# Three gate projections behind the context's norm, and the conditioning vector in the context's buffer

## The chip, the cores and the metric

The kernel runs on one core of a Trainium2 chip. The metric is the device time of one execution in microseconds (us). The engines of the core work side by side, each through its own list of instructions in order: TensorE (PE in the profile), VectorE (DVE), ScalarE (ACT), GpSimd (POOL) and SyncE (SP), which here only issues transfers. An instruction waits until what it needs has been written and until the buffer that it writes has been read for the last time.

## The reference, cut to what matters

One block of a diffusion transformer for 1024 tokens of width 1024, with a context of 256 tokens. The context is normalized and gives keys and values; the tokens give a long convolution, queries, keys, values and two gates, all from one weight matrix `w_in`.

```
ada   = silu(c) @ w_ada + b_ada                      # conditioning, 6 x 1024
hc    = modulate(rmsnorm(ctx, g_mix_pre), csh1, csc1)
kv_c  = hc @ w_in[:, OFF_K:OFF_G]                    # context keys and values
h     = modulate(rmsnorm(x, g_mix_pre), sh1, sc1)
proj  = h @ w_in
y_hy  = hyena_branch(proj[..., :OFF_Q], *hy_p) @ w_hy_up
q, k, v from proj; k_all = [k, k_c]; v_all = [v, v_c]
y_att = heads_out(diff_attention(q, k_all, v_all, lam)) @ w_att_up
g_hy, g_att = split(sigmoid(proj[..., OFF_G:]), 2)   # the gates: 2 x 1024 columns
mixed = (g_hy * y_hy + g_att * y_att) @ w_out
x = x + g1 * rmsnorm(mixed, g_mix_post); then the gated feed-forward layer
```

## The kernel before, in words

Matrices lie with their 128 rows of a tile on the partitions. A projection of 128 columns is a *tile* of `w_in`: `wload` (L126) loads 128x1024 weights from HBM (SP queue, L123), ScalarE casts them to the rounded form `whi`, VectorE subtracts to get the rest `wlo`, and `proj` (L136) does 24 matmuls per half of the tokens (8 each of `h_hi,whi`, `h_hi,wlo`, `h_lo,whi`). Buffers for `wraw`, `whi` and `wlo` are two each, so at most two tiles of weights are on their way. `raw_tile` (L486) projects one tile for both halves (48 matmuls) and stores it to HBM; the 16 gate tiles are such tiles (`graw`, tiles 24 to 39 of `win`).

The stages, by the time of the profile: the filter and the norm of the tokens (to 165 us), the Hyena convolutions (to about 525 us), the context stage (to about 614 us), the attention of four heads with the projections of the next head between (to about 1015 us), the mixing, the output and the feed-forward layer (to 1855 us).

Each of the four convolutions calls `filler` (L626) six times: in its forward transform twice, after the first and second product with the filter's spectrum, after finish(0) and finish(2), and after finish(1) and finish(3). Each call emits one tile. There are 24 tiles in the list, 8 of the convolution's own inputs and 16 gates, so the last three calls of the last convolution emit gate tiles 13, 14 and 15; the loop at L642 finds the list empty. `finish` (L578) does four matmuls, a copy by ScalarE (`yt`), four transposes and a product by VectorE into `u`. `hyena_out` (L605) casts `u` and stores it as `zs`.

The context stage (L743 to L772): `cx` is loaded on ScalarE's queue, squared and summed; `ss` sums over the partitions with TensorE (L170); VectorE forms the inverse root in twelve small operations and the diagonal `dg`; `bc` spreads it with TensorE (L184); VectorE multiplies and modulates `cx` and splits it into `c_hi` and `c_lo`. Then come q, k and v of head 0, the keys and values of the context for the four heads (24 matmuls of 256 columns each), and 15 conditioning tiles (`ada_tile`, L148): each loads 128x1024 of `w_ada` and reduces it against the vector `sc2` with one VectorE instruction. `sc2` is silu(c) on all partitions (`silu_bc`, L144). Context projections take their PSUM tile from a pool of two.

What sets the order is not the text alone: a scheduler orders each engine's instructions by its own costs, so that a tile that is written later can run earlier on its engine where nothing forbids it. SP's queue is one list too: a load that stands behind a store is issued only when the store's data is there.

Of the kernel before, what the change touches and what calls it, by code (L numbers as in the profile page):

```python
# [9 lines left out]
F32 = mybir.dt.float32  # L10
# [7 lines left out]
P = 128  # L18

L, D, C, DFF = 1024, 1024, 256, 2816  # L20
KD = D // P
# [12 lines left out]
NS, NTR = 3, 2  # L34
NHY = 6
FILL3 = ((10, 0), (1, 11), (2, 12), (3, 4, 5))
NGT = 16
NAB = 2
NGB = 12
UPO = (0, 0, 1, 1)  # L40
# [24 lines left out]
def block_kernel(tc, xT, ctxT, cvec, cT, wada1, wada, vecs, lamv, dbias, zT, fw1, fw2, fv, fw3, decay, mfs, mis, rope,  # L65
                 win, wup, wout, wgate, wupf, wdown, outT):
    nc = tc.nc
# [14 lines left out]
    def tt(out, a, b, op, eng=None):  # L82
        (eng or V).tensor_tensor(out=out, in0=a, in1=b, op=op)  # L83
# [7 lines left out]
    def act(out, in_, func, bias=0.0, scale=1.0, **k):  # L91
        A.activation(out=out, in_=in_, func=func, bias=bias, scale=scale, **k)

    def f(ap):
        return ap.bitcast(F32)

    def rawdma(out, in_, eng=None):
        (eng or nc.sync).dma_start(out=f(out) if out.dtype == F32R else out,
                                   in_=f(in_) if in_.dtype == F32R else in_)
# [4 lines left out]
    def pool(name, bufs=1, side=None, **k):  # L104
        return tc.tile_pool(name=name, bufs=bufs, side=side, **k)
# [20 lines left out]
    def wload(src, nk=8, neng=None):  # L126
        return wsplit(wload_raw(src, nk), nk, neng)
# [8 lines left out]
    def proj(ps, whi, wlo, xs, start=True, stop=True):  # L136
        n = len(xs)
        seq = [(whi, 0, k) for k in range(n)] + [(wlo, 0, k) for k in range(n)] + [(whi, 1, k) for k in range(n)]
        for i, (w, j, k) in enumerate(seq):
            T.matmul(out=ps, lhsT=w[:, k * P:(k + 1) * P], rhs=xs[k][j],  # L140
                     start=start and i == 0, stop=stop and i == len(seq) - 1)


    def silu_bc(dst, eng=None):  # L144
        (eng or nc.sync).dma_start(out=dst, in_=cvec.broadcast_to([P, D]))
        act(dst, dst, AF.Silu)
# [339 lines left out]
    def raw_tile(m, dst, ps_tile=None, gt_tile=None):  # L486
        whi, wlo = wload(win[m])
        for n in range(2):
            ps = ps_tile() if ps_tile else pacc.tile([P, 512], F32, tag="acc", name="ps")
            proj(ps, whi, wlo, hx[n])  # L490
            gt = gt_tile() if gt_tile else gpl.tile([P, 512], F32, tag="gt", bufs=2, name="gt")
            A.copy(out=gt, in_=ps)  # L492
            nc.sync.dma_start(out=dst[:, n * 512:(n + 1) * 512], in_=gt)
# [32 lines left out]
    matrices(mi, mis, lambda: yp.tile([P, 1024], F32, tag="hk", bufs=NHK, name="mraw"))  # L526

    def fftconv(u, o, c, p, filler):

        by_r = lambda t: t.rearrange("p h (a r) -> p h r a", r=8)  # L530
        S, D_ = quad(), quad()
        for r in (0, 2, 1, 3):
            pt = psf()
            for j, rr in enumerate((r, r + 4)):
                for h in range(2):
                    T.transpose(out=pt[:, j * 256 + h * P:j * 256 + (h + 1) * P], in_=by_r(u)[:, h, rr], identity=ident)
            ut = yp.tile([P, 512], F32, tag="ut", bufs=NUT, name="ut")
            A.copy(out=ut, in_=pt)
            pp = []
            for j in range(2):  # L540
                ps = psf()
                for part in range(2):
                    T.matmul(out=ps[:, part * 256:(part + 1) * 256], lhsT=mf[:, r + 4 * j, part],  # L543
                             rhs=ut[:, j * 256:(j + 1) * 256], start=True, stop=True)
                pp.append(ps)
            sd_from_psum(pp[0], pp[1], S, D_, SLOT[r])
            if r in (2, 3):
                filler()
# [14 lines left out]
        dft8_even(S, -1, Ze)  # L563
        times_k(Ze, 0)
        filler()
        Zo = quad()
        dft8_odd(D_, -1, Zo)
# [37 lines left out]
    def hyena_out(c, z):  # L605
        for h in range(2):
            hi = yp.tile([P, L], F32R, tag="hk", bufs=NHK, name="zhi")
            lo = yp.tile([P, L], F32R, tag="hk", bufs=NHK, name="zlo")
            A.copy(out=hi, in_=z[:, h])
            tt(lo, z[:, h], f(hi), ALU.subtract)  # L610
            rawdma(zs[0][c * 2 + h], hi)
            rawdma(zs[1][c * 2 + h], lo)
# [10 lines left out]

    tiles = [(m, praw[m]) for m in (2, 3, 6, 7, 8, 9, 10, 11)] + [(24 + j, graw[j]) for j in range(NGT)]

    def filler():  # L626
        raw_tile(*tiles.pop(0))

    u0 = part(0, 0)
    raws(4, 5)  # L630
# [8 lines left out]
    p11 = part(2, 1)  # L639
    fftconv(p01, 1, 1, p11, filler)  # L640
    hyena_out(1, p11)
    while tiles:  # L642
        filler()
    hy.close()
    fstack.close()

# [8 lines left out]
    def pacc_tile(name="ps"):  # L655
        if pc:
            return pc[0].tile([P, 512], F32, tag="acc", name=name)
        return psS.tile([P, 512], F32, tag="accb", bufs=NAB, name=name)
# [46 lines left out]
    def qk_tile(m, dst, ctx=None):  # L705
        whi, wlo = wload(win[m])
        for n in range(2):
            sl = slice(n * 512, (n + 1) * 512)
            ps = pacc_tile()
            proj(ps, whi, wlo, hx[n])  # L710
            sw = ap.tile([P, 512], F32, tag="raw", bufs=3, name="sw")
            V.stream_shuffle(out=sw, in_=ps, mask=swap)
            t1 = ap.tile([P, 512], F32, tag="t1", bufs=2, name="t1")
            tt(t1, ps, rp[:, 0, sl], ALU.mult)
            tt(sw, sw, rp[:, 1, sl], ALU.mult, RENG)
            tt(t1, t1, sw, ALU.add, RENG)
            hi = ap.tile([P, 512], F32R, tag="hl", bufs=6, name="qhi")
            lo = ap.tile([P, 512], F32R, tag="hl", bufs=6, name="qlo")
            A.copy(out=hi, in_=t1)
            tt(lo, t1, f(hi), ALU.subtract, RLENG)  # L720
            rawdma(dst[0][:, sl], hi)
            rawdma(dst[1][:, sl], lo)
        if ctx:
            ctx(0, whi, wlo)
# [12 lines left out]
    def qkv_parts(hd):  # L737
        return [lambda: qk_tile(12 + hd, [qs[0][hd], qs[1][hd]]),
                lambda: qk_tile(16 + hd, [ks[0][hd], ks[1][hd]]),
                lambda: v_tile(hd)]  # L740
# [1 line left out]

    cstk = contextlib.ExitStack()  # L743
    xp = cstk.enter_context(pool("ctx", side="right"))
    sc2 = xp.tile([P, D], F32, name="sc2")
    cx = xp.tile([P, KD, C], F32, name="cx")
    nc.scalar.dma_start(out=cx, in_=ctxT)
    silu_bc(sc2, nc.scalar)
    csq = xp.tile([P, KD, C], F32, name="csq")
    act(csq, cx, AF.Square)  # L750
    for k in (4, 2, 1):
# [8 lines left out]
        tt(c_lo[:, k], cx[:, k], f(c_hi[:, k]), ALU.subtract)  # L760
    chx = [(c_hi[:, k], c_lo[:, k]) for k in range(KD)]

    qk_tile(12, [qs[0][0], qs[1][0]])
    qk_tile(16, [ks[0][0], ks[1][0]], ctx_k)
    v_tile(0, ctx_v)
# [153 lines left out]
    for h in range(NH - 1):  # L919
        fill[h] = qkv_parts(h + 1)  # L920
    for j in range(NGT, 16):
        gt_tile = lambda: ap.tile([P, 512], F32, tag="raw", bufs=3, name="gt")
        fill[(j - NGT) % 3].append(lambda j=j: raw_tile(24 + j, graw[j], pacc_tile, gt_tile))
    LO[0] = G
# [549 lines left out]
```

## Time and profile before

| | |
|---|---|
| runs | 1862.24, 1858.52, 1862.54 us; median 1862.24 |
| the profiled execution | 1857.21 us, span 1855.4 us |
| mean granted clock of TensorE | 0.972 of full |
| TensorE busy | 1725.7 us, 93% of the span |
| VectorE busy | 1400.7 us, 75% |
| ScalarE busy | 757.0 us, 41% |
| transfers | 279.21 MB, mean 150 GB/s |

The granted clock is the share of full speed that the chip's throttle allowed TensorE. A row of the timeline gives the start, the length, the engine, the line and the operation of a run of equal instructions, and in brackets how long the engine stood idle before and what ended that.

### The profile page before, as it was taken

How to read it: one execution, taken by the hardware profiler on the slowest of the kernel's cores; microseconds unless marked ns; L12 is line 12 of the kernel's file. 1: busy time of each engine (PE TensorE's matmuls, PEld its weight loads, DVE VectorE, ACT ScalarE, POOL GpSimd, SP SyncE). 2: the span in 40 equal slices, each digit the busy share in tenths (PEclk: the TensorE clock that was granted, in tenths of full speed). 3: DMA queues.
4: the chain of work that ended last, by engine and by line, in shares of the span. 5: the costliest groups of instructions: out<-in, count | busy, mean ns of one | idle time of the engine just before them, and what ended most of it. 6: DMA issues, size and time to landing. Idle time of an engine off the chain costs nothing.

```text
span 1855.4 us, 22179 instructions
## 1 busy us (share of the span) xinstructions
PE 1725.7 (93%) x7902; PEld 1379.9 (74%) x7902; DVE 1400.7 (75%) x2478; ACT 757.0 (41%) x1193; POOL 65.2 (4%) x68
## 2 busy tenths in 40 slices
PE   7999989999997999999999987989999999798995
PEld 3587878787776887887877865768888887676874
DVE  5878777685958689898848588867776668777766
ACT  3411322222232466766755335533333335343421
POOL 0000000000000202110000000000000000000001
PEclk9899999999998999999999988999999999898998
DMA  9245533324276734337246753222352222534484
GB/s 333 95 171 188 175 124 127 98 91 153 85 252 219 224 91 151 123 106 252 86 176 199 271 171 131 101 96 95 112 178 94 75 90 80 169 102 149 140 283 161
DMA packets 122014, 279.21 MB, mean 150 GB/s; under 512 B 13699, under 2 KB 34959, under 8 KB 120624
## 3 DMA queue, kind: packets, MB, share of 16 engines
q1 hardware_dynamic: 115680, 270.14, 43.4%
q10 hardware_dynamic: 6224, 7.66, 1.4%
q8 instruction: 62, 1.02, 0.2%
q14 instruction: 48, 0.39, 0.1%
HBM read 202.25 MB, written 75.50 MB: 150 GB/s over the span
## 4 chain that ended last, share of the span: by engine, by line
PE 64%; DVE 21%; DMA 8%; issue 3%; ACT 2%; SPq 0%; DVEq 0%; ACTq 0%
PE pj L1121 27%; PE ps L140 19%; DVE pair L83 4%; PE S L810 4%; DVE quad L83 3%; DVE wlo L83 2%; PE pt L832 2%; PE psf L398 2%; PE psf L399 2%; PE psf L582 1%; DMA dacc_t<-dacc 1%; PE psf L543 1%; PE pv L841 1%; DMA wada_t<-wada 1%; PE psf L384 1%
## 5 line engine op out<-in xcount | busy, mean ns | idle before, releaser
L83 DVE TENSOR_TENSOR wlo<-wraw,whi 128x512 fp32r<-128x512 f32 (+2 forms) x199 | 167.3, 849 | 99.0 <-ACT whi L132 80.9
L1121 PE MATMUL pj<-hfc,whi 128*128 128x512 f32 x720 | 178.7, 390 | 0.0
L140 PE MATMUL ps<-h_hi,wlo 128*128 128x512 f32 x640 | 173.9, 401 | 0.7 <-DVE wlo L83 0.7
L140 PE MATMUL ps<-h_hi,whi 128*128 128x512 f32 x640 | 174.1, 403 | 0.0
L140 PE MATMUL ps<-h_lo,whi 128*128 128x512 f32 x640 | 166.8, 393 | 0.0
L1121 PEld LDWEIGHTS pj<-hfc,whi 128*128 128x128 f32 x720 | 135.3, 188 | 28.7
L1121 PE MATMUL pj<-hfb,whi 128*128 128x512 f32 x480 | 127.5, 410 | 11.8 <-ACT whi L1113 11.8
L140 PEld LDWEIGHTS ps<-h_hi,wlo 128*128 128x128 f32 x640 | 119.5, 190 | 24.9 <-DVE wlo L83 1.2
L140 PEld LDWEIGHTS ps<-h_hi,whi 128*128 128x128 f32 x640 | 120.0, 192 | 23.1
L140 PEld LDWEIGHTS ps<-h_lo,whi 128*128 128x128 f32 x640 | 119.0, 188 | 24.0
L1121 PE MATMUL pj<-hfa,whi 128*128 128x512 f32 x480 | 120.5, 394 | 4.9 <-ACT whi L1113 4.9
L1121 PEld LDWEIGHTS pj<-hfb,whi 128*128 128x128 f32 x480 | 94.0, 197 | 36.2 <-ACT whi L1113 13.4
L1113 ACT CAST whi<-wraw 128x512 fp32r<-128x512 f32 x120 | 72.4, 621 | 114.4 <-PE pj L1121 84.4
L1113 ACT CAST whi<-s 128x512 fp32r<-128x512 f32 x90 | 54.5, 620 | 140.4 <-DVE s L83 90.9
L810 PE MATMUL S<-KS,Q 128*128 128x512 f32 (+1 forms) x384 | 107.7, 374 | 3.1 <-DVE pr L814 2.7
L1121 PEld LDWEIGHTS pj<-hfa,whi 128*128 128x128 f32 x480 | 89.6, 188 | 26.8 <-ACT whi L1113 6.7
L492 ACT COPY gt<-ps 128x512 f32<-128x512 f32 x56 | 32.9, 587 | 187.3 <-PE ps L140 149.9
L132 ACT CAST whi<-wraw 128x1024 fp32r<-128x1024 f32 (+2 forms) x94 | 88.3, 940 | 51.2 <-PE ps L140 25.1
L1121 PE MATMUL pj<-hfc,wlo 128*128 128x512 f32 x360 | 97.1, 391 | 5.3 <-DVE wlo L83 5.3
L1121 PEld LDWEIGHTS pj<-hfc,wlo 128*128 128x128 f32 x360 | 67.3, 188 | 20.9 <-DVE wlo L83 7.0
L83 DVE TENSOR_TENSOR wlo<-s,whi 128x512 fp32r<-128x512 f32 x90 | 60.1, 686 | 27.3 <-PE pj L1121 27.3
L810 PEld LDWEIGHTS S<-KS,Q 128*128 128x128 f32 x384 | 64.4, 189 | 17.7 <-DVE pr L814 9.4
(472 smaller groups left out, 3456.9 us busy)
## 6 DMA issues: line engine op xcount, KB each, us to landing
wraw<-win SPq DMA_DIRECT2D x46, 512.0 KB, 3.7
wada_t<-wada SPq DMA_DIRECT2D x32, 512.0 KB, 10.2
wraw<-wgate SPq DMA_DIRECT2D x28, 512.0 KB, 3.2
wraw<-wupf SPq DMA_DIRECT2D x28, 512.0 KB, 3.2
araw<-ad SPq DMA_DIRECT2D x44, 256.0 KB, 3.5
w_ada<-wada SPq DMA_DIRECT2D x16, 512.0 KB, 7.4
kspec<-quad SPq DMA_DIRECT2D x8, 1024.0 KB, 3.9
kk<-kspec SPq DMA_DIRECT2D x16, 512.0 KB, 4.1
```

The lines of the kernel that those rows point to most:

```text
L83: (eng or V).tensor_tensor(out=out, in0=a, in1=b, op=op)
L132: A.copy(out=hi, in_=raw)
L140: T.matmul(out=ps, lhsT=w[:, k * P:(k + 1) * P], rhs=xs[k][j], start=start and i == 0, stop=stop and i == len(seq) - 1)
L384: T.matmul(out=ps, lhsT=a[:, cs], rhs=b, start=i == 0, stop=i == 2)
L398: T.matmul(out=out, lhsT=mfm(part, r), rhs=gen[r][:, 0:256], start=True, stop=False)
L399: T.matmul(out=out, lhsT=mfm(pb, rb), rhs=gen[rb][:, 256:512], start=False, stop=True)
L492: A.copy(out=gt, in_=ps)
L543: T.matmul(out=ps[:, part * 256:(part + 1) * 256], lhsT=mf[:, r + 4 * j, part], rhs=ut[:, j * 256:(j + 1) * 256], start=True, stop=True)
L810: T.matmul(out=S[:, :cn], lhsT=Q[j][:, i, qt * P:(qt + 1) * P], rhs=KS[i][:, c0:c0 + cn], start=j == 0, stop=j == 1)
L832: T.transpose(out=pt[:, b * 256 + qt * P:b * 256 + (qt + 1) * P], in_=av[qt][:, kt * P:(kt + 1) * P], identity=ident)
L1113: A.copy(out=hi, in_=src)
L1121: T.matmul(out=ps, lhsT=w[a][:, k * P:(k + 1) * P], rhs=xs[k][b], start=i == 0, stop=i == 11)
```

## The change

`filler` leaves the last `NGC` = 3 tiles in the list. They are emitted after the context's norm, before q of head 0. `sc2` is no longer a tile of its own: it is a slice of a tile with the tag of `cx` and one buffer, so it is loaded once `cx` has been read for the last time (the last `c_lo`), and `silu_bc` moves behind the norm's chain with it. All 15 conditioning reductions read `sc2` and follow it.

```diff
@@ -34,7 +34,7 @@
 NS, NTR = 3, 2
 NHY = 6
 FILL3 = ((10, 0), (1, 11), (2, 12), (3, 4, 5))
-NGT = 16
+NGT, NGC = 16, 3
 NAB = 2
 NGB = 12
 UPO = (0, 0, 1, 1)
@@ -624,7 +624,8 @@
     tiles = [(m, praw[m]) for m in (2, 3, 6, 7, 8, 9, 10, 11)] + [(24 + j, graw[j]) for j in range(NGT)]
 
     def filler():
-        raw_tile(*tiles.pop(0))
+        if len(tiles) > NGC:
+            raw_tile(*tiles.pop(0))
 
     u0 = part(0, 0)
     raws(4, 5)
@@ -639,8 +640,6 @@
     p11 = part(2, 1)
     fftconv(p01, 1, 1, p11, filler)
     hyena_out(1, p11)
-    while tiles:
-        filler()
     hy.close()
     fstack.close()
 
@@ -742,10 +741,8 @@
 
     cstk = contextlib.ExitStack()
     xp = cstk.enter_context(pool("ctx", side="right"))
-    sc2 = xp.tile([P, D], F32, name="sc2")
-    cx = xp.tile([P, KD, C], F32, name="cx")
+    cx = xp.tile([P, KD, C], F32, tag="cx", bufs=1, name="cx")
     nc.scalar.dma_start(out=cx, in_=ctxT)
-    silu_bc(sc2, nc.scalar)
     csq = xp.tile([P, KD, C], F32, name="csq")
     act(csq, cx, AF.Square)
     for k in (4, 2, 1):
@@ -760,6 +757,10 @@
         tt(c_lo[:, k], cx[:, k], f(c_hi[:, k]), ALU.subtract)
     chx = [(c_hi[:, k], c_lo[:, k]) for k in range(KD)]
 
+    sc2 = xp.tile([P, KD * C], F32, tag="cx", bufs=1, name="sc2")[:, 0:D]
+    silu_bc(sc2, nc.scalar)
+    for m, dst in tiles:
+        raw_tile(m, dst)
     qk_tile(12, [qs[0][0], qs[1][0]])
     qk_tile(16, [ks[0][0], ks[1][0]], ctx_k)
     v_tile(0, ctx_v)
```

Three places show what the order of the instructions becomes. The first is TensorE around the norm's matmuls: `h_` are matmuls of token tiles (gates and head 0), `c_` those of the context, `ss` and `bc` the norm's. Before:

```order
L140 MATMUL ps<-h_hi,whi 128x512 x3
L170 MATMUL ss<-ones,csq 128x1 x2
L140 MATMUL ps<-h_hi,whi 128x512 x5
L140 MATMUL ps<-h_hi,wlo 128x512 x8
L140 MATMUL ps<-h_lo,whi 128x512 x8
L184 MATMUL bc<-dg,ones 128x256
L140 MATMUL ps<-c_hi,whi 128x256 x3
L140 MATMUL ps<-h_hi,whi 128x512 x3
L140 MATMUL ps<-c_hi,whi 128x256 x3
```

The same place now:

```order
L140 MATMUL ps<-h_lo,whi 128x512 x3
L170 MATMUL ss<-ones,csq 128x1 x2
L140 MATMUL ps<-h_lo,whi 128x512 x5
L140 MATMUL ps<-h_hi,whi 128x512 x8
L140 MATMUL ps<-h_hi,wlo 128x512 x8
L140 MATMUL ps<-h_lo,whi 128x512 x6
L184 MATMUL bc<-dg,ones 128x256
L140 MATMUL ps<-h_lo,whi 128x512 x2
L140 MATMUL ps<-h_hi,whi 128x512 x8
L140 MATMUL ps<-h_hi,wlo 128x512 x8
L140 MATMUL ps<-h_lo,whi 128x512 x8
L140 MATMUL ps<-c_hi,whi 128x256 x8
```

From the last convolution's end to the first context matmul there are as many token matmuls as before, 176, but they fall differently: 155 ahead of `ss`, 21 between `ss` and `bc` and none between `bc` and `c_hi` before; 123, 27 and 26 now.

The second is TensorE in the end of the last convolution: `psf<-quad,mi` are the four matmuls of a `finish`, `psf<-ident,yt` its transposes, in the order finish(0), (2), (1), (3). Before:

```order
L582 MATMUL psf<-quad,mi 128x256 x4
L140 MATMUL ps<-h_hi,wlo 128x512 x4
L589 MATMUL psf<-ident,yt 128x128 x4
L140 MATMUL ps<-h_hi,wlo 128x512 x4
L140 MATMUL ps<-h_lo,whi 128x512 x8
L140 MATMUL ps<-h_hi,wlo 128x512 x8
L140 MATMUL ps<-h_lo,whi 128x512 x8
L582 MATMUL psf<-quad,mi 128x256 x4
```

The same place, finish(2) to finish(1), now:

```order
L582 MATMUL psf<-quad,mi 128x256 x4
L589 MATMUL psf<-ident,yt 128x128 x4
L140 MATMUL ps<-h_hi,wlo 128x512 x8
L582 MATMUL psf<-quad,mi 128x256 x2
L140 MATMUL ps<-h_lo,whi 128x512 x2
L582 MATMUL psf<-quad,mi 128x256 x2
```

Between the matmuls of finish(2) and those of finish(1) stood 32 gate matmuls; now eight stand there.

The third is SP's queue at the end of the context stage: `vs03`, `vs13`, `ks03` and `ks13` are the stores of the last context V and K tiles, `wraw_4360` the weights of that V tile, `wraw_4543` and `wraw_4863` those of head 1's q and k, `wada_t` conditioning tiles. Before:

```order
L123 DMA wraw_4360<-win 128x1024
L98 DMA vs11_139<-vl_4239 128x256
L98 DMA ks02_128<-kh_4275 128x256
L98 DMA ks12_132<-kl_4276 128x256
L123 DMA wraw_4543<-win 128x1024
L98 DMA vs02_136<-vh_4317 128x256
L123 DMA wraw_4863<-win 128x1024
L98 DMA vs12_140<-vl_4318 128x256
L98 DMA ks03_129<-kh_4354 128x256
L98 DMA ks13_133<-kl_4355 128x256
```

Now:

```order
L150 DMA wada_t_4438<-wada 128x1024
L98 DMA ks03_129<-kh_4354 128x256
L98 DMA ks13_133<-kl_4355 128x256
L150 DMA wada_t_4441<-wada 128x1024
L150 DMA wada_t_4444<-wada 128x1024
L98 DMA vs03_137<-vh_4396 128x256
L98 DMA vs13_141<-vl_4397 128x256
L150 DMA wada_t_4447<-wada 128x1024
L123 DMA wraw_4543<-win 128x1024
L123 DMA wraw_4863<-win 128x1024
```

The loads of head 1's weights moved from ahead of the last context K's stores to behind the stores of the last context V and a conditioning tile.

## Rows read from the trace of the kernel before

**Rows 1.** The page, busy time, share of the span and instructions of each engine.

```profile
PE 1725.7 (93%) x7902; PEld 1379.9 (74%) x7902; DVE 1400.7 (75%) x2478; ACT 757.0 (41%) x1193; POOL 65.2 (4%) x68
```

**Rows 2.** Table by stretches: length, busy of each engine (instructions), granted clock, DMA share, GB/s.

```profile
549.00:574.00 25.00, 9.40 (x32) 6.57 (x30) 23.98 (x49) 4.50 (x8) 4.57 (x3) 0.71 0.83 287
...
632.00:1000.00 368.00, 358.53 (x1985) 293.51 (x1986) 311.26 (x782) 246.11 (x381) 39.85 (x23) 1.00 0.47 151
...
566.00:580.00 14.00, 7.51 (x22) 5.90 (x23) 14.00 (x30) 2.83 (x8) 0.00 (x0) 0.50 0.62 210
...
596.00:614.00 18.00, 16.99 (x141) 16.39 (x139) 8.40 (x11) 7.94 (x14) 0.05 (x1) 1.00 0.76 234
```

**Rows 3.** What TensorE waited for, 500 to 632 us: total us, times, longest.

```profile
PE bc L184 <- DVE dg L89: 8.1, 1, 8.1
PE ps L140 <- ACT c_hi L759: 5.4, 1, 5.4
PE ss L170 <- DMA wada_t<-wada: 2.2, 1, 2.2
PE pt L680 <- ACT vT L702: 1.2, 1, 1.2
```

**Rows 4.** Timeline of TensorE.

```profile
507.33 0.66 PE L589 MATMUL psf<-ident,yt 128*128 128x128 f32 x4 [0.68 <-ACT yt L585]
...
510.47 0.60 PE L589 MATMUL psf<-ident,yt 128*128 128x128 f32 x4
...
552.40 2.31 PE L140 MATMUL ps<-h_hi,whi 128*128 128x512 f32 x5
...
557.06 2.00 PE L140 MATMUL ps<-h_lo,whi 128*128 128x512 f32 x8
567.13 1.22 PE L184 MATMUL bc<-dg,ones 128*128 128x256 f32 x2 [8.08 <-DVE dg L89]
573.71 1.23 PE L140 MATMUL ps<-c_hi,whi 128*128 128x256 f32 x3 [5.35 <-ACT c_hi L759]
...
580.51 1.11 PE L140 MATMUL ps<-c_lo,whi 128*128 128x256 f32 x8
581.46 2.00 PE L140 MATMUL ps<-h_hi,wlo 128*128 128x512 f32 x8
583.30 1.98 PE L140 MATMUL ps<-h_lo,whi 128*128 128x512 f32 x8
```

**Rows 5.** Timeline of VectorE.

```profile
513.12 1.22 DVE L83 TENSOR_TENSOR wlo<-wraw,whi 128x1024 fp32r<-128x1024 f32 x1
...
555.13 0.15 DVE L83 TENSOR_TENSOR rs_q<-rs,rs_m 128x2 f32<-128x2 f32 x1
...
559.77 0.69 DVE L83 TENSOR_TENSOR t<-ps,rp 128x512 f32<-128x512 f32 x1
...
563.07 1.28 DVE L151 CUSTOM_DVE_ANT_0 wada_t<-wada_t,sc,vec 128x1024 f32<-128x1024 f32 x1
...
569.41 2.28 DVE L83 TENSOR_TENSOR cx<-cx,bc 128x2048 f32<-128x2048 f32 x1
...
576.77 0.73 DVE L89 TENSOR_SCALAR cx<-cx,mcol,cols 128x256 f32<-128x256 f32 x2
```

**Rows 6.** Timeline of SP's queue and of ScalarE.

```profile
565.91 15.02 SPq L150 DMA_DIRECT2D wada_t<-wada  x7
...
606.98 0.33 SPq L123 DMA_DIRECT2D wraw<-win  x1
...
610.03 0.33 SPq L123 DMA_DIRECT2D wraw<-win  x1
...
612.83 1.04 ACT L132 CAST whi<-wraw 128x1024 fp32r<-128x1024 f32 x1 [2.27 <-DMA wraw<-win]
...
614.37 1.05 ACT L132 CAST whi<-wraw 128x1024 fp32r<-128x1024 f32 x1 [0.23 <-DMA wraw<-win]
```

**Rows 7.** The page, DMA issues: count, KB each, median us from issue to landing.

```profile
wraw<-win SPq DMA_DIRECT2D x46, 512.0 KB, 3.7
wada_t<-wada SPq DMA_DIRECT2D x32, 512.0 KB, 10.2
```

## The prediction

> **What bounds the kernel now.** I read the page's busy shares first. The PE row shows 93% of the span [rows 1], so TensorE sets the time except where it stands still, and the question is which standstills the change touches. The second view is the table by stretches. Between 549 and 574 us PE works 9.4 of 25.0 us, at a mean granted clock of 0.71. In the attention, 632 to 1000 us, it works 358.5 of 368.0 us [rows 2], so almost nothing can be gained there. Third, the waits of PE between 500 and 632 us: 8.1 us for the diagonal `dg` of the context's norm, 5.4 us for `c_hi`, 2.2 us before the row sum `ss`, 1.2 us for `vT` of the last context V tile [rows 3]. Fourth, the timeline shows what each wait costs afterwards: from 566 to 580 us the granted clock is 0.50, the lower of its two levels, 1.2 GHz instead of 2.4 [rows 2], and work that starts behind a wait is slow for a while.
>
> At the full clock eight context matmuls take 0.95 us (580.51 to 581.46) and eight 512-column ones 1.84 us (581.46 to 583.30) [rows 4], which makes 0.12 and 0.23 us each. The losses of before in this stage are then:
> - the wait before `ss`, 2.2 us [rows 3], and behind it 13 matmuls from 552.40 to 557.06, 4.7 us for 3.0 us of work [rows 4]: 1.7
> - the wait for `dg`, 8.1 [rows 3], and the broadcast matmul itself, 1.22 us [rows 4] for two passes of 0.12: 1.0
> - the wait for `c_hi`, 5.4 [rows 3], then 573.71 to 581.46 [rows 4], 7.75 us for 24 context and 8 other matmuls, 4.65 us of work: 3.1
> - the wait for `vT`, 1.2 [rows 3].
>
> Together 22.7 us. No matmul is added or removed, so the forecast is what these losses become.
>
> **The change part by part.** (1) *Fillers leave the last convolution.* Three of its last fillers do nothing now. The order shows finish(2) with no gate matmul ahead of its transposes, eight behind them, and then finish(1). An uncovered finish is seen in before: the first one waits 0.68 us for its `yt` copy [rows 4]. Then the eight `wlo` matmuls wait for VectorE: in before that subtraction starts at 513.12 us [rows 5], a `wlo` and a product, together 2.2 us, stand ahead of it no longer, so it ends near 512.1 us. The transposes, at 510.47 us for 0.6 us in before [rows 4], end near 510.5 us, since four matmuls less (0.9) and the 0.68 us nearly cancel. That is 1.6 us, and 0.4 us more for the first quad behind it. Sum 2.7, between 1 us (the subtraction comes in time) and 4.4 us (the clock falls as behind `ss`, 1.7).
>
> (2) *The start of the norm.* The context may only be loaded once the convolution's last z store has landed. With fewer matmuls in the convolution's end that comes earlier, but PE reaches `ss` after 32 fewer gate matmuls too (7.3 us, less the 2.7 lost). Both sides move forward by about 5 us, so I leave the wait at 2.2 and the slow work behind it at 1.7: 3.9, between 0 and 5.7 (the chain up to 1.8 us later).
>
> (3) *The norm's chain.* The sharing of the buffer makes the conditioning load wait until `cx` is read for the last time, so all 15 reductions of 1.28 us [rows 5] leave this chain; before, ten stood in it. Between `ss` and `dg` VectorE now does one shuffle, three more operations of 0.69, a `wlo` of 1.22 and twelve small ones of 0.15 to 0.2 us [rows 5], with `dg` about 6.5 us. PE has 27 matmuls there, 6.1 us at the full clock and 7.8 with the slow start: the 8.1 us wait and the 1.0 behind it go to 0 (at most 1.5). Between `bc` and the context matmuls stood no gate matmul before and 26 now, 5.9 us. VectorE needs, from 569.41 to the last `cx` product near 577.4 us [rows 5], 8.0 us less one reduction 1.2, plus a shuffle and a rope product of 0.6, plus 0.3 for the way: 8.3. Late is `c_hi` again, by 2.4, and I add 1.7 for the clock as behind `ss`: 4.1, between 1 and 6.
>
> (4) *The conditioning vector is late.* Its load starts with the last `c_lo`, and ScalarE's queue has the silu ahead of the `kh` copy that empties the PSUM tile of the first context K. Only two such tiles exist, so the second half of head 0's V waits for it. A load takes 4.1 to 5.9 us here (below), silu and reduction 2.3: the tile is empty 7 to 9.2 us after `c_lo`, PE is there after 8.1. I take 1.0, 0 to 2.
>
> (5) *The weights of the context stage.* SP issues a V tile's weights behind the stores of the K tile before. Two gaps of a tile's time arise; with 24 matmuls of 0.12 us per tile I put 1.0 on each of the last two V tiles: 2.0, between 0.5 and 6.
>
> (6) *Head 1's q weights.* This is what decides. Before, SP issues them two tiles ahead: issued at 606.98 us, ScalarE starts their cast at 612.83 us, having waited 2.27 us for the data, and the next pair 610.03 and 614.37 us [rows 6]. Now they stand behind the stores of the last context V tile and behind a conditioning tile, and PE's next work behind that tile's transposes is this q tile. From PE's last context matmul: `vT`, transposes, `vh`, `vl` about 1.8 us, three issues 0.8, 4.3 us from issue to cast (the second pair, whose cast waited hardly for anything else; the first makes 5.9), cast 1.05 [rows 6]: 8.0 us in place of the 1.2, between 6.6 (3.7 us, the median of these loads [rows 7], and the stores at once) and 14. Behind so long a wait the clock costs 3.1, as behind `c_hi` in before: 11.1.
>
> Sum after: 2.7 + 3.9 + 0 + 4.1 + 1.0 + 2.0 + 11.1 = 24.8, against 22.7: 2.1 us slower. The profiled execution took 1857.21 us (span 1855.4), which would become 1859.3; the median of the runs shown, 1862.24, lies 5.0 above it, and against that I forecast 1864.3 us. That is no change: 0.2%, 3.7 us, is about what a measurement of this kernel can tell.
>
> The conditioning tiles take 10.2 us to landing, a window's weights 3.7 [rows 7]. The Trainium skill, DMA: Bandwidth & Descriptors, "Queues, rings and completion order", says that SP's loads all share one row of rings and that each ring is consumed in order. By that rule q's weights, behind up to four conditioning tiles, would take nearer 10.2 than 4.3 us, and the sum would be 30.7. The 10.2 us agree with it for tiles queued in a row, seven in one stretch of 15 us [rows 6]; that a weight among them is held up, no row of before shows.
>
> **The rivals.** *B, faster.* The reductions were the whole stall and the loads come in time. The `ss` wait goes (0), the fillers cost 2.7, `c_hi` 2.4 + 1.7, vector and weights 1.0 together, q's weights 6.6 + 1.7: 16.1, so 6.6 us faster, 1855.6. For it: PE worked only 9.4 of 25 us there and has 53 matmuls to fill it with. Against it: it needs the lower end of three unknowns at once.
>
> *C, slower.* Conditioning tiles that were loaded during the convolution's end and the norm now travel among the context's stores and weights on SP's queue. If a weight behind them lands like one of them, in 10.2 us instead of 4.3 [rows 7], q's come 5.9 later, the last V's 2, and `vl` of the last tile, which stands on VectorE behind two reductions of tiles just issued, 2: 1864.3 + 9.9 = 1874. It decides against the forecast from a landing of about 6 us on. For it: the last five conditioning tiles are all issued in the last two tiles' time. Against it: SP spreads them now over the stage, and the queue moved 234 GB/s at 596 to 614 us [rows 2], less than at 549 to 574 (287).
>
> *D, the change doesn't do what it says.* The three tiles are written behind the chain, but in the order built their matmuls still come before the first context matmul, 176 in both; what is gained is only where the chain's pieces fall among them, while the order of the attention is dealt anew. There only 9.5 us stand idle in 368 [rows 2]; a third more of it would be 3: 1867.
>
> **How the numbers follow.** Forecast 0.42, own range 1860 to 1870, of which 0.26 is no change and 0.16 slower. B 0.30: 0.28 faster, 0.02 no change. C 0.20, slower. D 0.08, half and half. Faster 0.28, no change 0.32, slower 0.40. The range 1854 to 1874 goes from below B to C and leaves some 2 in 10 out.
>
> **What would show it.** In the profile after: no PE wait for `dg` over 1.5 us and a `c_hi` wait of about 2.4 show step 3; a wait of 1 to 2 us in front of the `wlo` matmuls behind finish(2) shows step 1; a PE wait of 6.6 us or more for `whi` of head 1's first q tile, just behind the last `pt<-ident,vT`, with a granted clock near 0.5 behind it, shows step 6. If that wait is under 3 us the forecast is wrong and B is right or too small. If it is over 12, or the context's K and V tiles wait more than 4 us in all, C is right. If the stretch from the last convolution to the first attention score is as long as forecast and the time is still another, the reason is in D.

## The result and the profile after

The changed kernel takes 1874.4 us (median of 9 runs, 1865.6 to 1878.3) against 1859.57 us for the kernel before (9 runs). The ratio is 1.0072, 95% interval [1.0059, 1.0086], which is 13.4 us of 1859.57; the two medians lie 14.8 us apart. The forecast was 1864.3 us and no change; the time lies at the edge of the range, 0.4 us above its upper end. The profiled execution took 1878.0 us, and that of before 1857.2: the two traces that are compared below lie 20.8 us apart, more than the medians.

The first view after is again the waits of TensorE, from 500 to 640 us (total us, times, longest), in answer to [rows 3]:

```profile
PE ps L140 <- ACT whi L132: 12.8, 3, 10.8
PE ss L170 <- DMA wada_t<-wada: 5.6, 1, 5.6
PE ps L140 <- DVE t L83: 2.4, 1, 2.4
```

The 8.1 us for `dg` are gone, and the 5.4 us for `c_hi` have become 2.4 us for `t` (the PSUM tile that the context's first matmul needs). In their place stand 10.8 us for one `whi`, and the wait before `ss` has grown from 2.2 to 5.6 us. The releaser named for `ss` is a conditioning tile's transfer; it is not what TensorE needed, which is the sum over the context's squares; their time is shown further below, with the run that loads the context on SP's queue.

The timeline of TensorE, in answer to [rows 4]: first the end of the last convolution, then `ss`, `bc` and the context's first matmul, then the end of the context stage.

```profile
507.62 1.97 PE L582 MATMUL psf<-quad,mi 128*128 128x256 f32 x8 [0.66 <-DVE quad L83]
510.27 0.66 PE L589 MATMUL psf<-ident,yt 128*128 128x128 f32 x4 [0.68 <-ACT yt L585]
...
513.33 0.66 PE L589 MATMUL psf<-ident,yt 128*128 128x128 f32 x4 [0.68 <-ACT yt L585]
515.08 2.14 PE L140 MATMUL ps<-h_hi,wlo 128*128 128x512 f32 x8 [1.10 <-DVE wlo L83]
517.40 1.10 PE L582 MATMUL psf<-quad,mi 128*128 128x256 f32 x4 [0.19 <-DVE quad L86]
...
553.81 0.99 PE L170 MATMUL ss<-ones,csq 128*128 128x1 f32 x4 [5.65 <-DMA wada_t<-wada]
554.66 2.48 PE L140 MATMUL ps<-h_lo,whi 128*128 128x512 f32 x5
...
563.75 0.59 PE L184 MATMUL bc<-dg,ones 128*128 128x256 f32 x2
...
564.65 2.01 PE L140 MATMUL ps<-h_hi,whi 128*128 128x512 f32 x8
...
572.64 1.19 PE L140 MATMUL ps<-c_hi,whi 128*128 128x256 f32 x8 [2.35 <-DVE t L83]
...
613.15 0.44 PE L679 MATMUL pt<-ident,vT 128*128 128x128 f32 x2 [0.46 <-ACT vT L701]
624.35 3.78 PE L140 MATMUL ps<-h_hi,whi 128*128 128x512 f32 x8 [10.76 <-ACT whi L132]
627.92 2.52 PE L140 MATMUL ps<-h_hi,wlo 128*128 128x512 f32 x8
630.28 2.00 PE L140 MATMUL ps<-h_lo,whi 128*128 128x512 f32 x8
632.11 1.98 PE L140 MATMUL ps<-h_hi,whi 128*128 128x512 f32 x8
```

The same ends of the context stage before:

```profile
504.69 1.97 PE L582 MATMUL psf<-quad,mi 128*128 128x256 f32 x8 [0.66 <-DVE quad L83]
...
614.20 0.44 PE L680 MATMUL pt<-ident,vT 128*128 128x128 f32 x2 [1.21 <-ACT vT L702]
614.39 2.08 PE L140 MATMUL ps<-h_hi,whi 128*128 128x512 f32 x8
```

The context stage, from the first finish of the last convolution (504.69 us before, 507.62 after) to the last context transposes (614.20, 613.15), is 4.0 us shorter: 105.5 against 109.5. What follows takes it all back and more. The q tile of head 1 starts 11.2 us after those transposes, where it followed at 0.2 us before, and its first 24 matmuls take 7.8 us (624.35 to 632.11) where 5.4 are their work. Of the 20.8 us between the two traces, 2.9 lie ahead of the first finish, the stage gives 4.0 back, the attention up to its last transposes takes 19.3 more (the wait for q's weights and the slow matmuls behind it included), and what follows it 2.6 more.

Why the weights came so late is read on SP's queue, VectorE and ScalarE, in answer to [rows 6]:

```profile
611.22 1.04 SPq L150 DMA_DIRECT2D wada_t<-wada  x2
614.03 0.33 SPq L98 DMA_DIRECT2D vs<-vh  x1
615.90 0.33 SPq L98 DMA_DIRECT2D vs<-vl  x1
616.28 0.42 SPq L150 DMA_DIRECT2D wada_t<-wada  x1
616.76 0.92 SPq L123 DMA_DIRECT2D wraw<-win  x2
...
614.24 1.29 DVE L151 CUSTOM_DVE_ANT_0 wada_t<-wada_t,sc,vec 128x1024 f32<-128x1024 f32 x1 [1.74 <-DMA wada_t<-wada]
615.45 0.42 DVE L83 TENSOR_TENSOR vl<-pt,vh 128x256 fp32r<-128x256 f32 x1
...
623.25 1.04 ACT L132 CAST whi<-wraw 128x1024 fp32r<-128x1024 f32 x1 [9.25 <-DMA wraw<-win]
```

The load is issued at 616.76 us, behind the store of `vl`. `vl` itself waited on VectorE: a conditioning reduction stands ahead of it, and that one's tile landed 1.74 us after VectorE was free. From the issue to the cast 6.5 us pass, where before it was 4.3 to 5.9 [rows 6].

The table by stretches, in answer to [rows 2]: the norm's chain, then the stretch with the q tile.

```profile
549.00:574.00 25.00, 17.84 (x70) 14.55 (x71) 20.23 (x49) 6.32 (x12) 2.56 (x2) 0.80 0.32 120
...
614.00:650.00 36.00, 25.41 (x102) 19.91 (x103) 18.34 (x46) 8.99 (x12) 7.29 (x4) 0.81 0.78 239
```

TensorE works 17.8 of 25 us in the first, where it was 9.4 before, and the granted clock of 0.81 in the last row shows what the wait there costs behind it.

### The profile page after: what moved, and what is told of

Same layout as the page of the kernel before. It is cut to its first block, busy times and chain, and to the rows that moved or that the text cites. A ratio compares the mean times of both kernels' runs of the same rounds, so it can differ in the third digit from the quotient of the medians.

```text
span 1876.2 us, 22188 instructions
## 1 busy us (share of the span) xinstructions
PE 1736.1 (93%) x7902; PEld 1388.8 (74%) x7902; DVE 1401.2 (75%) x2478; ACT 757.1 (40%) x1193; POOL 70.1 (4%) x68
## 4 chain that ended last, share of the span: by engine, by line
PE 60%; DVE 22%; DMA 10%; issue 3%; ACT 2%; SPq 1%; DVEq 0%; POOL 0%; ACTq 0%
PE pj L1122 26%; PE ps L140 17%; DVE pair L83 4%; DVE quad L83 3%; PE S L811 3%; DMA wada_t<-wada 2%; PE pt L833 2%; PE psf L398 2%; PE psf L399 2%; DVE wlo L83 2%; DMA dacc_t<-dacc 1%; PE psf L543 1%; PE pv L842 1%; PE psf L384 1%; DMA wraw<-win 1%
## 5 line engine op out<-in xcount | busy, mean ns | idle before, releaser
L140 PE MATMUL ps<-h_hi,whi 128*128 128x512 f32 x640 | 173.4, 404 | 10.8 <-ACT whi L132 10.8
L140 PE MATMUL ps<-h_lo,whi 128*128 128x512 f32 x640 | 170.8, 398 | 0.0
```

## The experiments

Theory 1: the late weights of head 1's q are the loss. Theory 2: the order of the attention, dealt anew, loses as much. Theory 3: conditioning tiles ahead in SP's rings delay any weight. All ratios below are to the kernel before as measured beside each run; its medians there were 1857.5 to 1859.4 us.

**Early q weights.** The changed kernel, with the load of head 1's q weights emitted earlier, together with the last context V's weights. The lines that do it (`qk_tile` then takes the weights that are loaded already):

```diff
-        ctx_v(hd, *wload(win[20 + hd]))
+        hl_ = wload(win[20 + hd])
+        if hd == NH - 1:
+            early[13] = wload_raw(win[13])
+        ctx_v(hd, *hl_)
```

> The changed kernel, but the load of head 1's q weights is emitted with the last context V's weights, so that SP issues it two stores and four conditioning tiles earlier; everything else is as changed. Theory 1 (the late q weights are the loss): PE's wait in front of head 1's q falls from 10.8 us to under 2, the slow clock behind it goes, about 12 us come back, some 1862 us. Theory 2 (the attention, whose order was dealt anew, loses as much as the context stage): the wait goes, but the time falls by 6 us or less, to about 1868. Theory 3 (SP's ring is full of conditioning tiles, so any weight there is late): the load is issued earlier and lands later, the wait stays above 5 us, 1870.

Measured: 1858.3 us, ratio 1.0001 [0.9990, 1.0013]. TensorE from the last context transposes on:

```profile
613.23 0.44 PE L679 MATMUL pt<-ident,vT 128*128 128x128 f32 x2 [1.61 <-ACT vT L701]
613.42 2.08 PE L140 MATMUL ps<-h_hi,whi 128*128 128x512 f32 x8
615.42 2.11 PE L140 MATMUL ps<-h_hi,wlo 128*128 128x512 f32 x8
```

The wait is gone and the whole loss with it: theory 1 holds (it expected 1862 us), and theory 3's wait above 5 us did not come. The order of the attention is another again in this kernel, so that it does not separate what the wait costs from what the order there costs. What the stage had won (613.23 less 507.81, 105.4 us, as in the changed kernel) does not show in the total either. One trace can't place a gain of that size: ahead of the first finish TensorE does the same work in all kernels here, and yet that finish begins anywhere between 504.7 us (the trace of before, the earliest) and 511.1 us.

**The shared buffer alone** (`NGT, NGC = 16, 0`).

> Only the shared buffer: no filler is left over (NGC = 0), the conditioning vector takes the context's buffer. q of head 1 is again behind the last V's stores in SP's queue. Theory 1: the loss belongs to the buffer, 1868 to 1876 us, with a PE wait of 8 to 11 us in front of q of head 1. Theory 2 (the moved tiles or the new order): no slower than 1862.

Measured: 1868.0 us, ratio 1.0058 [1.0039, 1.0078]. The wait in front of head 1's q:

```profile
610.53 0.44 PE L679 MATMUL pt<-ident,vT 128*128 128x128 f32 x2 [0.46 <-ACT vT L701]
619.75 3.78 PE L140 MATMUL ps<-h_hi,whi 128*128 128x512 f32 x8 [8.79 <-ACT whi L132]
```

It is the shared buffer, not the moved tiles, that puts the weights behind the stores. The likely reason, which no run shows by itself: the buffer makes the conditioning tiles late, and the scheduler places the weights, which are emitted after them, at their end. The stage is also shorter (506.43 to 610.53, 104.1 us) than with the moved tiles.

**The moved tiles alone.** `sc2` has its own buffer and stands where it was; three tiles follow the norm. Two of the changed lines (`cx` and `silu_bc` too are as before the change):

```diff
-    sc2 = xp.tile([P, KD * C], F32, tag="cx", bufs=1, name="sc2")[:, 0:D]
+    sc2 = xp.tile([P, D], F32, name="sc2")
```

> Only the moved tiles: three gate tiles behind the context's norm, the conditioning vector in a buffer of its own and emitted where it was. q of head 1 is issued ahead of the last V's stores, as before. Theory 1: no wait there, the norm's stall filled with 53 gate matmuls: 1850 to 1858 us. Theory 2: the uncovered finish and the new order of the attention cost as much as is won: 1860 to 1867.

Measured: 1863.3 us, ratio 1.0031 [1.0018, 1.0045]. The expectation of a gain fell. The stage takes 510.93 to 621.79, 110.9 us: the `ss` wait is 4.9 us, `c_hi` is waited for 4.9 us in three pieces, and the finish is uncovered. These 1.4 us over before explain a part; 4 us stay open. In that trace they lie ahead of 510 us, where the instructions of TensorE are the same. The time lies in theory 2's range, but the attention takes 328.2 us as before, so its order is not where the time went. The wait before `ss` belongs to these tiles: 4.9 us here, 1.5 us with the shared buffer alone.

**Late q weights in the kernel before.** A copy of one column makes that load wait for the last `vl` (the three lines that do it):

```diff
+    early[13] = wp.tile([P, 8 * P], F32, tag="wraw", bufs=2, name="wraw")
+    V.tensor_copy(out=early[13][:, 0:1], in_=f(last_vl[0][:, 0:1]))
+    nc.sync.dma_start(out=early[13], in_=win[13])
```

> The kernel before with one thing made late: the load of head 1's q weights waits for the rest (vl) of the last context V (one VectorE copy of one column stands between). Theory 1: PE waits 6 to 9 us in front of q of head 1 and runs slowly behind it, 7 to 11 us in all: 1867 to 1870 us. Theory 2: the attention makes up for it or it hides: within 3 us of before.

Measured: 1877.6 us, ratio 1.0107 [1.0086, 1.0128], 20 us, twice what was expected. The load and its cast (no conditioning tile is near), and the q tile:

```profile
616.40 0.42 SPq L775 DMA_DIRECT2D wraw<-win  x1
...
621.60 1.04 ACT L132 CAST whi<-wraw 128x1024 fp32r<-128x1024 f32 x1 [6.12 <-DMA wraw<-win]
...
622.70 3.78 PE L140 MATMUL ps<-h_hi,whi 128*128 128x512 f32 x8 [7.62 <-ACT whi L132]
```

The position alone is enough: 7.6 us of wait. The load takes 5.2 us without conditioning tiles, against 6.5 in the changed kernel and 5.3 with the shared buffer alone (613.34 to 618.66 us there), so theory 3 is worth about 1 us at most; a run below takes only 3.4 us with conditioning tiles ahead. The other half of the loss comes later: the waits of the scores for `pr` from 614 to 1000 us are 8.1 us in 8 pieces, 2.7 in four before. k's weights also moved back in this kernel (cast at 647.03 us, before at 625.83), so the 20 us are not q's alone.

**A second trace of the changed kernel.**

> The changed kernel once more, for a second trace. If the 2.9 us wait for yr in head 3 and the slow clock behind it belong to its order, they are there again; if they are chance, the attention is 5 to 6 us shorter than in the first trace. The wait in front of head 1's q is 9 to 11 us by every theory.

Measured: 1872.5 us in the one run. The wait in front of q is 11.2 us and that for `yr` in head 3 1.9 us (2.9 in the first trace):

```profile
624.80 3.78 PE L140 MATMUL ps<-h_hi,whi 128*128 128x512 f32 x8 [11.21 <-ACT whi L132]
...
882.30 1.65 PE L140 MATMUL ps<-z,whi 128*128 128x512 f32 x3 [1.86 <-DVE yr L86]
```

The wait for `yr` is there again, so it is not the chance of one trace. From the last context transposes to the last transposes of the attention it is 346.1 us here, 347.5 in the first trace, 328.2 before. Of the 18 to 19 us more, the q wait and its clock make 13 to 14; 4 to 6 lie in the attention, at `yr` and the slow clock behind it. The shared buffer alone has nearly the same order there and 340.0 us, 0.5 more than its q wait and clock, so the order by itself does not cause it. In both traces of the changed kernel VectorE's product into `yr` waits for the load of `yr` there, 3.4 and 2.4 us; why that load is late stays open. Over all kernels, the attention takes 340 to 350 us where head 1's q weights are late and 327 to 332 us where they are not.

**The shared buffer with early q weights.**

> Only the shared buffer (NGC = 0), and head 1's q weights emitted with the last context V's weights. If the late q weights are the whole loss of the shared buffer, their wait of 8.8 us and the slow 2.3 us go and the 5 us that this context stage is shorter than before (104.1 against 109.5 us from the last convolution's first finish to the last context transposes) remain: 1852 to 1855 us, faster than before. If what the stage wins is given back in the attention, as with the moved tiles and early q weights, the time is that of before, 1857.

Measured: 1858.2 us, ratio 1.0005 [0.9991, 1.0019]. The loss goes again and no gain is left, though the stage takes only 505.94 to 608.56, 102.6 us. The attention takes 331.6 us to its last transposes, 3.4 more than before; a `pt` wait of 2.5 us stands there, and what is behind the attention was 3.7 us longer in that trace. Why so little remains is not settled.

**The context on SP's queue, ahead of the conditioning tiles,** on top of the early q weights:

```diff
-    nc.scalar.dma_start(out=cx, in_=ctxT)
+    nc.sync.dma_start(out=cx, in_=ctxT)
```

> The changed kernel with early q weights, and the context loaded on SP's queue, ahead of the conditioning tiles, instead of ScalarE's. Theory: the context's load was slow (10 us from issue to the square) because five conditioning tiles travelled beside it, and with it ahead of them PE's wait in front of the row sum falls from 5.2 us to under 2.5, 2 to 5 us less in all, 1853 to 1856 us. Rival: the load lasts as long wherever it is queued, or its issue behind the gate stores makes up for it; then the wait stays at 5 us and the time at 1858.

Measured: 1852.7 us, ratio 0.9962 [0.9944, 0.9980]: faster than both kernels. The context's load and its square, before:

```profile
538.11 0.35 ACTq L747 DMA_DIRECT2D cx<-ctxT  x1
545.67 1.92 ACT L92 ACTIVATE csq<-cx 128x2048 f32<-128x2048 f32 x1 [4.10 <-DMA cx<-ctxT]
```

in the changed kernel:

```profile
538.28 0.35 ACTq L745 DMA_DIRECT2D cx<-ctxT  x1
548.30 1.91 ACT L92 ACTIVATE csq<-cx 128x2048 f32<-128x2048 f32 x1 [7.80 <-DMA cx<-ctxT]
```

and in this one, with the rest of the norm:

```profile
537.91 0.33 SPq L747 DMA_DIRECT2D cx<-ctxT  x1
...
544.55 1.92 ACT L92 ACTIVATE csq<-cx 128x2048 f32<-128x2048 f32 x1 [4.40 <-DVE sw L713]
...
549.49 0.58 PE L170 MATMUL ss<-ones,csq 128*128 128x1 f32 x4 [0.90 <-ACT qhi L720]
556.96 0.70 PE L184 MATMUL bc<-dg,ones 128*128 128x256 f32 x2 [0.87 <-DVE dg L89]
565.35 0.71 PE L140 MATMUL ps<-c_hi,whi 128*128 128x256 f32 x2 [0.94 <-ACT c_hi L758]
```

The load took 10.0 us to its use on ScalarE's queue and at most 6.6 on SP's; whether the queue itself or its place ahead of the conditioning tiles did it, this run does not separate. The `ss` wait falls to 0.9 us, the clock is at 1.00 from 549 to 574 us, and the stage takes 507.36 to 607.69, 100.3 us.

**The same without the moved tiles.**

> Shared buffer alone, early q weights, and the context loaded on SP's queue ahead of the conditioning tiles. PE's wait in front of the row sum was 1.5 us in the kernel with the shared buffer alone, so only 0 to 2 us can be won over the run without this: 1851 to 1855 us by the first theory, 1857 if the attention gives it back.

Measured: 1856.9 us, ratio 0.9987 [0.9974, 1.0000]; no `ss` wait, stage 102.2 us. Here `c_hi` is waited for 3.5 us, since no gate matmul stands between `bc` and it. With the moved tiles it was 1852.7 us, so they seem to be worth something once the chain starts in time; the intervals of the two ratios just overlap.

**The changed kernel with the context on SP's queue alone.**

> The changed kernel with one difference: the context loaded on SP's queue ahead of the conditioning tiles; head 1's q weights stay behind the last V's stores. If the two losses are separate, the wait in front of the row sum goes (5.4 to about 1 us) and the one in front of head 1's q stays at 9 to 12 us: 4 to 6 us less than the changed kernel, 1867 to 1870 us. If the late q weights hang on the late start of the norm, their wait falls below 6 us and the time to 1862.

Measured: 1864.9 us, ratio 1.0028 [1.0013, 1.0042]. The `ss` wait is 1.3 us; the wait for head 1's q fell to 5.8 us, less than the 9 expected, but the last V tile's weights are late by 2.3 us now, 9.4 us in all for `whi`. The load of q's weights and its cast, and the q tile:

```profile
615.35 0.93 SPq L123 DMA_DIRECT2D wraw<-win  x2
...
618.79 1.04 ACT L132 CAST whi<-wraw 128x1024 fp32r<-128x1024 f32 x1 [4.32 <-DMA wraw<-win]
...
619.89 3.78 PE L140 MATMUL ps<-h_hi,whi 128*128 128x512 f32 x8 [5.83 <-ACT whi L132]
```

The load is issued 1.7 us after the last context transposes begin (3.6 in the changed kernel) and its cast starts 3.4 us later (6.5). By the mark set in advance, a wait below 6 us, the late q weights hang in part on the late start of the norm; the time lies between the two that were expected. In the total the two losses nearly add up: early q weights give 0.71% and this load 0.44%, and both together 1.10%.

**The kernel before with the context on SP's queue.**

> The kernel before with the context loaded on SP's queue ahead of the conditioning tiles, nothing else. If the gain of the run with early q weights and this load comes from this load alone, it is faster than before by 4 to 7 us, 1852 to 1855. If the load was in time here already (PE's wait in front of the row sum was 2.2 us, and the conditioning reductions still stand in the norm's chain), 0 to 2 us are won: 1857 to 1859, and the shared buffer is what lets the rest be won.

Measured: 1860.9 us, ratio 1.0012 [0.9998, 1.0027]. Nothing is won. The conditioning reductions still hold the chain (`dg` 9.4 us), and the wait before `ss` grew from 2.2 to 3.8 us, because ScalarE does the silu of the conditioning vector ahead of the square here, and that waits for its own load:

```profile
549.82 1.06 ACT L92 ACTIVATE sc<-sc 128x1024 f32<-128x1024 f32 x1 [4.22 <-DMA sc<-cvec]
550.78 1.90 ACT L92 ACTIVATE csq<-cx 128x2048 f32<-128x2048 f32 x1
```

Before, the square came first (545.67 us). So this run does not show what the earlier load is worth by itself. It shows that the load alone gains nothing in this kernel; with the shared buffer the silu stands behind the norm and can't hold the square. No run has the load and the moved tiles without the shared buffer.

## Why the prediction was right or wrong

The direction of the sum was right (2.1 us slower), its size was not (13.4), so that no change was forecast where the kernel is slower. Two terms were too small, those of steps 2 and 6, and the attention, which was put at nothing, took 4 to 6 us more. By steps:

- **Step 1**, the last convolution's end, 2.7 us. Measured 0.68 + 1.10 + 0.19 = 2.0, at the places named.
- **Step 2**, the start of the norm, 3.9 us (between 0 and 5.7). Measured 5.6 of wait and 3.1 of slow clock behind it (554.66 to 564.65 us, 10.0 us for 29 gate matmuls and `bc`, 6.9 of work; granted clock 0.70): 8.7. This step failed. Both sides were to come earlier by the same. Counted from the last convolution's first finish, TensorE is at `ss` 4.6 us earlier than before, but the context's load is issued only 2.8 us earlier, and it lasted 10.0 us to its use against 7.6; the chain behind it is 0.8 shorter. The length goes with the transfers beside it: in the traces that load the context on ScalarE's queue it is 6.6 and 6.9 us with three conditioning tiles issued on SP's within 5 us, 7.4 and 7.6 with four, and 9.3 to 10.0 with five. With the load on SP's queue the `ss` wait falls to 1.3 us and 0.44% come back, though q's weights come earlier there too.
- **Step 3**, the chain: the wait for `dg` went to 0 as forecast. That before the context matmuls is 2.35 (2.4 forecast), but it is another wait, and that the numbers agree is luck: `c_hi` is cast from 567.66 us on, and what TensorE waits for is the PSUM tile that a rope product of VectorE, between the products of `cx`, reads last:

```profile
567.66 1.05 ACT L756 CAST c_hi<-cx 128x256 fp32r<-128x256 f32 x3 [5.90 <-DVE cx L89]
...
571.81 0.68 DVE L83 TENSOR_TENSOR t<-ps,rp 128x512 f32<-128x512 f32 x1
```

The clock stayed high behind it in this trace (0.3 us lost instead of 1.7). In the second trace of the changed kernel the wait is the same and the clock falls: 24 context matmuls take 4.4 us instead of 2.8, about the 1.7 us that were forecast.

```profile
571.01 1.65 PE L140 MATMUL ps<-c_hi,whi 128*128 128x256 f32 x8 [2.37 <-DVE t L83]
```

- **Step 4**, the late conditioning vector, 1.0: nothing. The silu came at 578.12 us, and no wait of TensorE for the PSUM tile stands behind it.
- **Step 5**, the weights of the last V tiles, 2.0: 1.55 + 0.54 = 2.1.
- **Step 6**, head 1's q weights, 11.1 us: 0.46 + 10.76 + 2.3 of slow clock (7.8 less 5.4) = 13.5. The mechanism and its place were right: the kernel without this wait has lost nothing. Too small were the time until the issue (4.1 us from the last context matmul, 612.69 to 616.76 us, instead of 2.6: `vl` stands behind a reduction, the bound that had gone to rival C) and the way from issue to cast (6.5 instead of 4.3); the clock cost less (2.3 instead of 3.1).

The measured terms add up to 29.0 us against 22.7 before, 6.3 slower where 2.1 were forecast. In the two traces the stretch from the first finish to the end of q's first 24 matmuls is 9.0 us longer; the rest of that lies in pieces of under half a microsecond. The attention adds its 4 to 6 us, which the forecast put at nothing because only 9.5 us stood idle there.

Rival C named the two additions of step 6 and the time that came. By its own marks it is not right: the wait is 10.8 us, not over 12, and the context's K and V tiles wait 2.1 us for their weights, not over 4. Its mechanism, a weight that lands like the conditioning tiles ahead of it, is the smaller part, since the same load takes 5.2 us without any conditioning tile near and 3.4 to 6.7 us with some; the 234 and 287 GB/s that stood against it are those of all transfers of the core, not of SP's queue. That its sum met the time is in part luck, as it left step 2 at 3.9 us and the attention at nothing. Rival D named another 3 us in the attention; 4 to 6 stand there, at `yr`, and their cause is open. Rival B was wrong: the `ss` wait grew and q's weights came late. The 0.40 for slower was the largest of the three chances, yet the likeliest single case was no change. The terms of steps 2 and 6 were taken inside their bounds as if they had nothing to do with each other; the run with the context on SP's queue, where both waits shrink, suggests that they have.

## What to carry to other kernels

When a change makes a group of loads late, look in each queue for what is emitted after them: a scheduler that keeps the order will push those back too, and a prefetch that sat two tiles ahead becomes a wait at the next tile. Read a wait's length from the place of the load in its queue, with everything that must be stored ahead of it, before pricing the stall that the change is meant to fill. The stall that is filled and the prefetch that is lost are two changes, and can be had one by one.

## What the runs showed of the hardware

A load of 1 MB issued on ScalarE's queue took 10.0 us to its use while five conditioning tiles of 512 KB were issued on SP's within 5 us of it; on SP's, ahead of those tiles and at nearly the same moment, at most 6.6. After a wait of 10.8 us TensorE's first eight 512-column matmuls took 3.6 us (624.35 to 627.92), twice their 1.8, at a granted clock of 0.50, and the third eight were at full speed again. A wait of 2.4 us went either way in the same kernel: behind 2.35 us in one trace the granted clock was 1.00 (572.64 to 577.60 us), behind 2.37 us in the other 0.69 (571.01 to 576.50 us).
